# Lower parts of split weights by an adding DMA instead of a subtraction on VectorE or GpSimd

## The chip, the cores and the metric

The kernel runs on one core of a Trainium2 chip. The metric is device microseconds of one execution, the median of three runs. Beside the runs there is one profiled execution, from which the page and the trace come.

## What is computed

One layer of an encoder trunk on x of 512 x 1024 in float32: a token mixer with two branches (stick-breaking attention with 8 heads of 64, and a diagonal state-space branch, S5), their gated merge and an output projection, a layer norm, a SwiGLU channel mixer and a second layer norm. Every sub-layer is shifted, scaled and gated by vectors that come from c and w_ada. Cut to what matters:

```python
mod = silu(c) @ w_ada + b_ada              # six vectors of 1024
h = normalize(x) * (1 + sc_m) + sh_m
q, k, v, u, g_sb, g_ssm = split(h @ w_in)  # 3 x 512, 512, 2 x 1024
y_sb  = stick_breaking_attention(q, k, v) @ w_sb_up
y_ssm = s5_branch(u, ..., w_glu, b_glu) @ w_ssm_up
y = (sigmoid(g_sb) * y_sb + sigmoid(g_ssm) * y_ssm) @ w_out
x = layer_norm(ALPHA * x + (1 + g_m) * y, ln1_g, ln1_b)
h = normalize(x) * (1 + sc_f) + sh_f
gate, up = split(h @ w_ffn_in)
x = layer_norm(ALPHA * x + (1 + g_f) * (silu(gate) * up @ w_ffn_out), ln2_g, ln2_b)
```

## The kernel before

Each float32 matrix product is made of three passes in the shorter type float32r (`mm3`, L149 is its matmul). Every operand is split into an upper part, the value rounded to float32r, and a lower part, what the rounding left; the passes are upper by upper, upper by lower and lower by upper.

A weight piece of 128 x 1024 (512 KB) is a unit. `unit()` (L170) takes one of eight raw buffers, loads it on SyncE's queue, casts it on ScalarE into an upper part `whi` (L177) and subtracts the two into a lower part `wlo` (`sub`, L159) on the engine it is given. There are four `whi` and four `wlo` buffers. `slot_unit()` (L181) does the same by halves of 128 x 512 into s slots through `split()` (L164 is its cast). Which engine subtracts is written by hand: GpSimd (G) for the q and k tiles (`qk_tile`), the v tiles (`v_tiles`) and the gate tiles (`gate_tile`); VectorE (V, the default) for w_glu and the two up projections; by the table `ENG` for the twelve pieces of w_out that are split (four halved ones, and four whole ones in each of two passes over the rows), and by `FENG` for the first pairs of the channel mixer, which are two units and two halved ones. The pieces of w_ffn_out are split on VectorE; later pieces of w_ffn_in are split by `operand()` (L1049 its cast).

The stages, by the time of the profiled run: up to about 92 us the ramp, with the six vectors, the norm of x and its transposes into h (L362, L367, L368), the state-space setup (L469 among it) and the first gates; 92 to 206 us the state-space scan (L555 to L558 build the ce tiles from s tiles, L614 and L595 clear tiles, L637 to L652 are the scan) and the q, k and v tiles; 206 to 340 us attention and gate tiles (L244 accumulates the six vectors from w_ada); 340 to 350 us the copies of y (L839) and their split; 350 to 404 us the glu and the up projections; 404 to 435 us the first pass of the output projection (L916 scales rows of x on GpSimd); 435 to 472 us the first layer norm (L943, L950, L283, L284) beside the second pass; then the channel mixer and the second norm.

Each instruction belongs to a stream with a priority, in this order: first, feed, ssm, qkv, later, attn, gates, mix, ffn. Weight pieces are in feed. A scheduler places all instructions on their engines by these priorities and by its own times, so an edit of an operation moves others too. Loads keep the order of the program. Within an engine instructions run in the order placed.

Of the kernel before, what the change touches and what calls it, by code (L numbers as in the profile page):

```python
# [17 lines left out]
ALU = mybir.AluOpType  # L18
# [39 lines left out]
TAIL = 256  # L58

ENG, FENG = "VGVVVGVGGGGVVGGG", "GGGV"  # L60

# [20 lines left out]
def _build(tc, I, out):  # L82
# [75 lines left out]
    def sub(dst, a, b, eng=V):  # L158
        return eng.tensor_tensor(dst, a, b, ALU.subtract)  # L159

    def split(x, n=512, eng=V, keep=False):

        h, l = get(F32R), get(F32R)
        acopy(h[:, :n], x[:, :n])  # L164
        sub(l[:, :n], x[:, :n], h[:, :n], eng)
        if not keep:
            put(x)
        return h, l

    def unit(view, a, b, eng=V):  # L170

        with prio("feed"):
            raw = wp.tile([P, D], F32, tag="raw", name=nm("raw"), bufs=NRAW)
            load(raw.rearrange("p (a b) -> p a b", a=a), view)
            hi = wp.tile([P, D], F32R, tag="whi", name=nm("whi"), bufs=NHI)
            lo = wp.tile([P, D], F32R, tag="wlo", name=nm("wlo"), bufs=NHI)
            acopy(hi, raw)  # L177
            sub(lo, raw, hi, eng)
        return hi.rearrange("p (a b) -> p a b", a=a), lo.rearrange("p (a b) -> p a b", a=a)

    def slot_unit(view, a, b, eng=V):  # L181

# [335 lines left out]

    def fm_one(view, h, K=KC, o=None, eng=V):

        w = unit(view, K, P, eng) if K == KC else view
        o = fbank() if o is None else o
        for kc in range(K):
            mm3(o, [x[:, kc, :] for x in w], h[kc], kc == 0, kc == K - 1)
        return o
# [142 lines left out]
    def qk_tile(i):  # L668
        o = fm_one(w_in[:, :, 256 + P * i:256 + P + P * i], hT, eng=G)
        if i < 2:  # L670
# [4 lines left out]
    def v_tiles(i):  # L675
        us = [unit(w_in[:, k:k + 4, 1024 + 256 * i:1280 + 256 * i], 4, 256, G) for k in (0, 4)]
        for m2 in range(2):
# [17 lines left out]

    def gate_tile(i, eng):
        lst = (gs, gb)[i // 8]
        o = fm_one(gate_w(i), hT, eng=eng)
        with prio("feed"):
# [94 lines left out]
    for hp in range(4):  # L794
# [20 lines left out]
        for a in range(2):  # L815
# [3 lines left out]
            for g in range(2):  # L819
                i = 4 * hp + 2 * a + g  # L820
                with prio("gates"):
                    gate_tile(i, G)
                later(("gate", i))
# [74 lines left out]
    with prio("mix"):  # L898
# [10 lines left out]
        def proj(blocks):  # L909
# [7 lines left out]
            for k in range(KC):  # L917
                view, eng = w_o[:, k:k + 1, :], (V, G)[ENG[k + 8 * (blocks[0] // 2)] == "G"]
                if k >= KEEP:
                    wo[k] = [[x[:, 0, h * 512:(h + 1) * 512] for x in w] for w in [unit(view, 1, D, eng)] for h in range(2)]  # L920
                elif k not in wo:
                    wo[k] = slot_unit(view, 1, D, eng)
                later(("out", blocks[0] // 2 * 8 + k))
# [73 lines left out]
    with prio("ffn"):  # L997
        first, wx = [], []
        for i in range(FIRST):
            for c in (0, FH):  # L1000
                view = w_f[:, :, c + P * i:c + P * i + P]
                if len(first) < 2:
                    w = unit(view, KC, P, (V, G)[FENG[len(first)] == "G"])
                    w = [[x[:, k, :] for x in w] for k in range(KC)]
                else:
                    pair = slot_unit(view, KC, P, (V, G)[FENG[len(first)] == "G"])
                    wx += pair
# [171 lines left out]
        for kc in range(NF - LAST):  # L1179
            if kc == len(acts):  # L1180
                parts((kc - FIRST) // 2)
            w = unit(w_d[:, kc:kc + 1, :], 1, D)
            for m in range(NT):
# [6 lines left out]
        for kc in range(NF - LAST, NF):  # L1190
# [3 lines left out]
            if kc < NF - NHI:  # L1194
                ws[kc] = slot_unit(view, 1, D)
                order.append(kc)
            else:
                w = unit(view, 1, D)
                ws[kc] = [[x[:, 0, h * 512:(h + 1) * 512] for x in w] for h in range(2)]
# [88 lines left out]
```

## Time and profile before

| | |
|---|---|
| median of three runs | 841.67 us (841.38 to 842.21) |
| profiled execution | 841.87 us, its span 840.2 us |
| TensorE (PE) busy | 760.7 us (91%), granted clock 0.966 of full speed |
| VectorE (DVE) busy | 637.8 us (76%) |
| ScalarE (ACT) busy | 416.7 us (50%) |
| GpSimd (POOL) busy | 190.9 us (23%) |
| chain that ended last | PE 61%, DVE 24%, issue 4%, ACT 4%, DMA 4% |

The rows further below are of four views: the page (busy times, costliest groups, DMA issues), busy time by stage, and the timeline of an engine. In a timeline a line is a run of equal instructions (x tells how many), with its start, its time, and in brackets how long the engine was idle before it and what ended that.

### The profile page before, as it was taken

The numbers are of one execution on the slowest core, as the hardware profiler recorded it, in microseconds if no ns is written. First come the engines' busy times: TensorE is split into PE (matmuls) and PEld (weight loads), VectorE is DVE, ScalarE is ACT, GpSimd is POOL, SyncE is SP. The second block draws the span as 40 slices with busy tenths as digits, with TensorE's granted clock in tenths as the row PEclk, the third lists the DMA queues.
The fourth block names the chain that finished last, engine by engine and source line by source line (L and its number), as shares of the span: only waits on it lengthen the run. The fifth ranks groups of instructions, "written<-read, shape, count | busy, mean of one in ns | idle before, by whom it ended". The sixth has DMA issues, their size and how long they took to land.

```text
span 840.2 us, 12264 instructions
## 1 busy us (share of the span) xinstructions
PE 760.7 (91%) x4767; PEld 667.5 (79%) x4767; DVE 637.8 (76%) x975; ACT 416.7 (50%) x689; POOL 190.9 (23%) x161
## 2 busy tenths in 40 slices
PE   3969896899999888699998589999999999999995
PEld 2858686897888577588886589999999999888884
DVE  5599778789677998688879988767778777533267
ACT  4234623454887665883526294444445556632211
POOL 1451626662532443100464000000000000000013
PEclk9989999899999999899999699999999999999998
DMA  9960004420002471770972003414445334441001
GB/s 275 354 176 26 1 1 136 116 76 26 1 1 83 147 228 53 240 251 28 348 238 87 0 2 102 150 52 151 151 152 181 116 107 150 148 154 48 1 26 75
DMA packets 95754, 97.86 MB, mean 116 GB/s; under 512 B 4040, under 2 KB 85968, under 8 KB 95696
## 3 DMA queue, kind: packets, MB, share of 16 engines
q1 hardware_dynamic: 95552, 96.82, 36.6%
q8 instruction: 37, 0.61, 0.3%
q10 hardware_dynamic: 144, 0.26, 0.1%
q14 instruction: 21, 0.17, 0.1%
HBM read 94.97 MB, written 2.10 MB: 116 GB/s over the span
## 4 chain that ended last, share of the span: by engine, by line
PE 61%; DVE 24%; issue 4%; ACT 4%; DMA 4%; SPq 2%; POOL 1%; POOLq 0%; DVEq 0%; ACTq 0%
PE b L149 60%; DVE s L244 3%; DVE s L159 2%; SPq L146 2%; DVE s L469 1%; DMA s<-w_in 1%; DMA ra<-w_ada 1%; DVE s L621 1%; DVE wlo L159 1%; DVE raw L1042 1%; ACT s L424 1%; DVE s L642 1%; DVE s L402 1%; DVE st L280 1%; ACT s L425 1%
## 5 line engine op out<-in xcount | busy, mean ns | idle before, releaser
L149 PE MATMUL b<-h,whi 128*128 128x256 f32 (+1 forms) x896 | 217.4, 332 | 18.8 <-DVE h L159 9.4
L159 DVE TENSOR_TENSOR wlo<-raw,whi 128x1024 fp32r<-128x1024 f32 x103 | 129.5, 1264 | 69.1 <-ACT whi L177 37.1
L149 PEld LDWEIGHTS b<-h,whi 128*128 128x128 f32 x896 | 151.2, 191 | 33.4 <-DVE h L159 9.6
L149 PE MATMUL b<-s,whi 128*128 128x256 f32 (+1 forms) x800 | 166.7, 307 | 6.7 <-ACT whi L177 6.7
L149 PE MATMUL b<-h,wlo 128*128 128x256 f32 (+1 forms) x448 | 147.9, 331 | 0.0
L149 PEld LDWEIGHTS b<-s,whi 128*128 128x128 f32 x800 | 129.5, 190 | 16.6 <-ACT whi L177 7.0
L149 PE MATMUL b<-whi,s 128*128 128x512 f32 (+1 forms) x392 | 122.5, 390 | 0.0
L149 PE MATMUL b<-s,wlo 128*128 128x256 f32 (+1 forms) x400 | 121.2, 305 | 0.8 <-DVE wlo L159 0.8
L159 DVE TENSOR_TENSOR s<-s,s 128x512 fp32r<-128x512 f32 (+4 forms) x112 | 89.2, 802 | 37.0 <-PE b L149 18.1
L1049 ACT CAST whi<-raw 128x1024 fp32r<-128x1024 f32 x70 | 72.7, 1050 | 75.5 <-PE b L149 43.3
L177 ACT CAST whi<-raw 128x1024 fp32r<-128x1024 f32 x66 | 68.9, 1048 | 80.9 <-PE b L149 66.2
L159 POOL TENSOR_TENSOR wlo<-raw,whi 128x1024 fp32r<-128x1024 f32 x33 | 84.5, 2572 | 63.5 <-ACT whi L177 62.7
L149 PEld LDWEIGHTS b<-h,wlo 128*128 128x128 f32 x448 | 85.6, 191 | 7.2 <-POOL wlo L159 0.4
L1228 POOL TENSOR_TENSOR s<-s,s 128x512 f32<-128x512 f32 x6 | 8.6, 1431 | 356.6 <-DVE s L1227 356.6
L149 PE MATMUL b<-s,s 128*128 128x128 f32 (+2 forms) x438 | 81.9, 317 | 6.1 <-DVE s L159 3.8
L149 PEld LDWEIGHTS b<-whi,s 128*128 128x128 f32 x392 | 73.3, 188 | 16.6
L164 ACT CAST s<-s 128x512 fp32r<-128x512 f32 (+1 forms) x106 | 57.8, 570 | 49.4 <-DVE s L744 13.7
L149 PEld LDWEIGHTS b<-s,s 128*128 128x128 f32 x438 | 68.8, 192 | 15.9 <-DVE s L159 4.4
L149 PEld LDWEIGHTS b<-s,wlo 128*128 128x128 f32 x400 | 75.3, 188 | 4.5 <-DVE wlo L159 1.0
L149 PE MATMUL b<-wlo,s 128*128 128x512 f32 (+1 forms) x196 | 76.5, 390 | 0.0
L244 DVE SCALAR_TENSOR_TENSOR s<-ra,ca,s 128x256 f32<-128x256 f32 x88 | 58.3, 681 | 2.8 <-DMA ra<-w_ada 2.2
L159 POOL TENSOR_TENSOR s<-s,s 128x512 fp32r<-128x512 f32 (+1 forms) x32 | 39.5, 1246 | 78.9 <-ACT s L164 56.1
(244 smaller groups left out, 1111.8 us busy)
## 6 DMA issues: line engine op xcount, KB each, us to landing
raw<-w_ffn_in SPq DMA_DIRECT2D x44, 512.0 KB, 4.3
ra<-w_ada SPq DMA_DIRECT2D x32, 512.0 KB, 6.0
raw<-w_in SPq DMA_DIRECT2D x26, 512.0 KB, 4.7
raw<-w_ffn_out SPq DMA_DIRECT2D x22, 512.0 KB, 3.4
wa<-w_ada SPq DMA_DIRECT2D x12, 512.0 KB, 7.7
raw<-w_out SPq DMA_DIRECT2D x12, 512.0 KB, 6.3
s<-x SPq DMA_DIRECT2D x16, 256.0 KB, 4.2
wa<-w_ada SPq DMA_DIRECT2D x8, 256.0 KB, 4.9
```

Source lines behind the costliest of these rows:

```text
L146: return tc.keep_in_program_order(nc.sync.dma_start(out=o, in_=i))
L149: return nc.tensor.matmul(o, lhsT, rhs, start=start, stop=stop, skip_group_check=True, **kw)
L159: return eng.tensor_tensor(dst, a, b, ALU.subtract)
L164: acopy(h[:, :n], x[:, :n])
L177: acopy(hi, raw)
L244: stt(dst, r_, ca[:, k:k + 1], init if k == 0 else dst, ALU.mult, ALU.add)
L280: V.bn_stats(st[:, i, :], x)
L402: e.scalar_tensor_tensor(p_, n, -c, p_, ALU.mult, ALU.add)
L424: act(o, a, AF.Abs, bias=b)
L425: sins.append(act(o, o, AF.Sin, scale=-1.0, bias=hpi_c))
L1049: acopy(hi, x)
L1228: G.tensor_tensor(z[h], z[h], l2b[h], ALU.add)
```

## The change

A lower part is no longer raw minus upper part on VectorE or GpSimd. ScalarE writes the negated value, rounded to float32r as the upper part is, into the lower part's buffer, and a DMA issued from GpSimd adds the raw piece onto it. This is the default of `unit()` and `slot_unit()`; only w_ffn_out keeps the subtraction on VectorE, and so do `operand()` and all splits of activations, on the engines that they had. The two tables go.

```diff
-ENG, FENG = "VGVVVGVGGGGVVGGG", "GGGV"
...
+    def lower(l, x, h, eng):
+
+        if eng is None:
+            act(l, x, AF.Copy, scale=-1.0)
+            G.dma_start(out=l, in_=x, accum_op=ALU.add)
+        else:
+            sub(l, x, h, eng)
+
     def split(x, n=512, eng=V, keep=False):
 
         h, l = get(F32R), get(F32R)
         acopy(h[:, :n], x[:, :n])
-        sub(l[:, :n], x[:, :n], h[:, :n], eng)
+        lower(l[:, :n], x[:, :n], h[:, :n], eng)
...
-    def unit(view, a, b, eng=V):
+    def unit(view, a, b, eng=None):
...
             acopy(hi, raw)
-            sub(lo, raw, hi, eng)
+            lower(lo, raw, hi, eng)
...
-    def slot_unit(view, a, b, eng=V):
+    def slot_unit(view, a, b, eng=None):
...
-            w = unit(w_d[:, kc:kc + 1, :], 1, D)
+            w = unit(w_d[:, kc:kc + 1, :], 1, D, V)
...
-                ws[kc] = slot_unit(view, 1, D)
+                ws[kc] = slot_unit(view, 1, D, V)
...
-                w = unit(view, 1, D)
+                w = unit(view, 1, D, V)
```

46 units and 12 halves are concerned. The order of the loads on SyncE is the same. Elsewhere the scheduler places instructions anew; three places follow. In the names, numbers are buffers and versions; L147 is the matmul's line after the change, L149 before.

On TensorE at the first v tile (about 131 us; whi_261 and its wlo are the unit's parts, h0 and h1 the split of h), before:

```order
L149 MATMUL b4_70<-ce_179_1096,s23_185_1112 128x128
L149 MATMUL b4_70<-ce_180_1098,s16_186_1113 128x128
L149 MATMUL b7_73<-whi_261_1545,h0_64 128x256
L149 MATMUL b6_72<-whi_261_1545,h0_64 128x256
L149 MATMUL b7_73<-wlo_262_1546,h0_64 128x256
L149 MATMUL b7_73<-whi_261_1545,h1_65 128x256
L149 MATMUL b7_73<-whi_261_1545,h0_64 128x256
```

and after:

```order
L147 MATMUL b4_70<-ce_179_1098,s23_185_1114 128x128
L147 MATMUL b4_70<-ce_180_1100,s16_186_1115 128x128
L147 MATMUL b7_73<-whi_261_1551,h0_64 128x256
L147 MATMUL b6_72<-whi_261_1551,h0_64 128x256
L591 MATMUL b4_70<-ident_95,s3_136_861 128x128 x4
L147 MATMUL b7_73<-wlo_262_1552,h0_64 128x256
L147 MATMUL b7_73<-whi_261_1551,h1_65 128x256
L147 MATMUL b7_73<-whi_261_1551,h0_64 128x256
```

A row of four transposes (L591) has moved in between the first upper-part matmuls and the first one of the lower part.

On ScalarE at the start of the glu (whi_551, 560, 569 and 572 are the upper parts of the two w_glu pieces and of the first two up pieces, L839 or L845 the copies of y), before:

```order
L164 CAST s50_544_3254<-s42_535_3224 128x512
L773 COPY s40_461_2821<-b4_70 64x256
L164 CAST s48_548_3262<-s30_537_3238 128x512
L164 CAST s34_532_3208<-s40_461_2821 128x512
L177 CAST whi_551_3268<-raw_550_3266 128x1024
L177 CAST whi_560_3312<-raw_559_3310 128x1024
L177 CAST whi_569_3356<-raw_568_3354 128x1024
L177 CAST whi_572_3390<-raw_571_3388 128x1024
L847 ACT_TABLE_LOAD
```

and after:

```order
L845 COPY s41_536_3257<-b2_68 128x4x128
L845 COPY s30_537_3264<-b3_69 128x4x128
L183 CAST whi_560_3339<-raw_559_3337 128x1024
L162 ACTIVATE wlo_561_3340<-raw_559_3337 128x1024
L170 CAST s34_532_3234<-s40_461_2843 128x512
L183 CAST whi_569_3384<-raw_568_3382 128x1024
L162 ACTIVATE wlo_570_3385<-raw_568_3382 128x1024
L170 CAST s50_544_3280<-s42_535_3250 128x512
L170 CAST s45_546_3284<-s41_536_3257 128x512
L170 CAST s48_548_3288<-s30_537_3264 128x512
L183 CAST whi_572_3419<-raw_571_3417 128x1024
L162 ACTIVATE wlo_573_3420<-raw_571_3417 128x1024
```

Before, all copies and casts of y stand ahead of the first upper part; now whi_551 and its negated copy, the two rows just ahead of these, come before three copies of y, and three casts of y come after the third pair. On TensorE, at the same place, before:

```order
L149 MATMUL b6_72<-s23_542_3250,whi_560_3312 128x512
L149 MATMUL b6_72<-s39_543_3251,whi_560_3312 128x512
L149 MATMUL b7_73<-s23_542_3250,whi_560_3312 128x512
L149 MATMUL b7_73<-s39_543_3251,whi_560_3312 128x512
L149 MATMUL b4_70<-s23_542_3250,wlo_552_3269 128x512
L149 MATMUL b4_70<-s50_544_3254,whi_551_3268 128x512
L149 MATMUL b4_70<-s6_545_3255,whi_551_3268 128x512
L149 MATMUL b4_70<-s50_544_3254,wlo_552_3269 128x512
```

and after:

```order
L147 MATMUL b6_72<-s23_542_3276,whi_560_3339 128x512
L147 MATMUL b6_72<-s39_543_3277,whi_560_3339 128x512
L147 MATMUL b7_73<-s23_542_3276,whi_560_3339 128x512
L147 MATMUL b7_73<-s39_543_3277,whi_560_3339 128x512
L147 MATMUL b2_68<-s25_329_2113,whi_572_3419 128x512
L147 MATMUL b2_68<-s9_330_2114,whi_572_3419 128x512
L147 MATMUL b3_69<-s25_329_2113,whi_572_3419 128x512
L147 MATMUL b3_69<-s9_330_2114,whi_572_3419 128x512
L147 MATMUL b4_70<-s23_542_3276,wlo_552_3295 128x512
L147 MATMUL b4_70<-s50_544_3280,whi_551_3294 128x512
```

Four matmuls on the fourth upper part, whi_572, now stand ahead of the first one on the lower part wlo_552.

On ScalarE at the first layer norm (mv_677 is its first statistic, whi_663 to whi_672 pieces of w_out), before:

```order
L177 CAST whi_666_3941<-raw_665_3939 128x1024
L177 CAST whi_669_3947<-raw_668_3945 128x1024
L283 ACTIVATE mv_677_4060<-mv_677_4060,cst_102 128x1
L177 CAST whi_672_3953<-raw_671_3951 128x1024
L284 ACTIVATE mv_677_4060<-mv_677_4060 128x1
```

and after:

```order
L183 CAST whi_663_3983<-raw_662_3981 128x1024
L162 ACTIVATE s20_721_4343<-raw_717_4335 128x512
L162 ACTIVATE wlo_667_3991<-raw_665_3988 128x1024
L183 CAST whi_666_3990<-raw_665_3988 128x1024
L162 ACTIVATE wlo_670_3998<-raw_668_3995 128x1024
L183 CAST whi_669_3997<-raw_668_3995 128x1024
L162 ACTIVATE wlo_673_4005<-raw_671_4002 128x1024
L183 CAST whi_672_4004<-raw_671_4002 128x1024
L289 ACTIVATE mv_677_4112<-mv_677_4112,cst_102 128x1
L290 ACTIVATE mv_677_4112<-mv_677_4112 128x1
L953 ACTIVATE s29_675_4108<-s29_675_4108,mv_677_4112 128x512
```

Three more negated copies and one of a half now stand ahead of the first step on mv_677.

## Rows read from the trace of the kernel before

**Rows 1.** The page: busy time, share of the span and instructions of each engine.
```profile
PE 760.7 (91%) x4767; PEld 667.5 (79%) x4767; DVE 637.8 (76%) x975; ACT 416.7 (50%) x689; POOL 190.9 (23%) x161
```

**Rows 2.** Busy time by stage: from:to, length, engines, granted clock, DMA share, GB/s.
```profile
92.00:206.00 114.00, 99.32 (x635) 89.35 (x634) 95.03 (x141) 47.75 (x87) 61.23 (x52) 0.94 0.23 65
...
350.00:435.00 85.00, 85.00 (x373) 68.60 (x372) 69.62 (x107) 42.13 (x61) 18.00 (x9) 0.98 0.71 233
...
460.00:472.00 12.00, 0.50 (x2) 0.30 (x2) 12.00 (x19) 3.25 (x9) 1.93 (x5) 0.61 0.15 44
```

**Rows 3.** The page's groups: lower parts and upper parts; busy us, mean ns, idle.
```profile
L159 DVE TENSOR_TENSOR wlo<-raw,whi 128x1024 fp32r<-128x1024 f32 x103 | 129.5, 1264 | 69.1 <-ACT whi L177 37.1
...
L177 ACT CAST whi<-raw 128x1024 fp32r<-128x1024 f32 x66 | 68.9, 1048 | 80.9 <-PE b L149 66.2
L159 POOL TENSOR_TENSOR wlo<-raw,whi 128x1024 fp32r<-128x1024 f32 x33 | 84.5, 2572 | 63.5 <-ACT whi L177 62.7
```

**Rows 4.** Timeline, ramp; start, us, engine, operation, idle before in brackets.
```profile
49.28 7.82 DVE L469 TENSOR_SCALAR s<-s,s 128x128 f32<-128x128 f32 x5
...
57.88 1.11 PE L362 MATMUL b<-ident,s 128*128 128x128 f32 x4 [6.01 <-DVE s L368]
...
58.52 0.67 DVE L469 TENSOR_SCALAR s<-s,s 128x128 f32<-128x128 f32 x3
...
59.03 0.78 ACT L367 ACTIVATE h<-b,sc 128x512 fp32r<-128x512 f32 x1 [6.24 <-PE b L362]
```

**Rows 5.** Timeline, state-space part: v tiles and a wait for L558.
```profile
131.75 4.89 POOL L159 TENSOR_TENSOR wlo<-raw,whi 128x1024 fp32r<-128x1024 f32 x2 [0.44 <-ACT whi L177]
...
134.16 0.39 PE L149 MATMUL b<-wlo,h 128*128 128x256 f32 x1 [1.50 <-POOL wlo L159]
...
134.31 2.88 DVE L637 TENSOR_TENSOR s<-s,s 128x512 f32<-128x512 f32 x1
...
147.57 0.69 DVE L647 TENSOR_TENSOR s<-s,s 128x512 f32<-128x512 f32 x1
...
147.59 1.11 PE L578 MATMUL b<-ident,s 128*128 128x128 f32 x4 [4.37 <-DVE s L558]
```

**Rows 6.** Timeline, attention, VectorE and TensorE.
```profile
297.95 3.45 DVE L159 TENSOR_TENSOR s<-s,s 64x512 fp32r<-64x512 f32 x2
...
301.45 0.56 PE L149 MATMUL b<-s,s 128*128 128x256 f32 x3 [3.40 <-DVE s L159]
...
302.29 1.38 DVE L159 TENSOR_TENSOR s<-s,s 64x512 fp32r<-64x512 f32 x2
```

**Rows 7.** Timeline, start of the glu, ScalarE and TensorE.
```profile
340.88 2.90 ACT L839 COPY s<-b 128x512 f32<-128x512 f32 x3
...
348.16 1.04 ACT L177 CAST whi<-raw 128x1024 fp32r<-128x1024 f32 x1 [0.21 <-DMA raw<-w_glu]
...
349.26 3.78 PE L149 MATMUL b<-s,whi 128*128 128x512 f32 x8 [6.70 <-ACT whi L177]
352.84 0.63 PE L149 MATMUL b<-s,wlo 128*128 128x512 f32 x1
```

**Rows 8.** Timeline, output projection, GpSimd.
```profile
423.17 3.92 POOL L916 TENSOR_SCALAR s<-s 128x512 f32<-128x512 f32 x2
```

**Rows 9.** Timeline, first layer norm, VectorE.
```profile
437.05 2.28 DVE L943 SCALAR_TENSOR_TENSOR s<-s,s 128x512 f32<-128x512 f32 x1
...
456.99 2.69 DVE L159 TENSOR_TENSOR h<-s,h 128x512 fp32r<-128x512 f32 x1
...
466.67 0.68 DVE L159 TENSOR_TENSOR s<-raw,s 128x512 fp32r<-128x512 f32 x1
467.26 0.68 DVE L943 SCALAR_TENSOR_TENSOR s<-s,s 128x512 f32<-128x512 f32 x1
```

**Rows 10.** The page's DMA issues: count, KB each, median us to landing.
```profile
raw<-w_ffn_out SPq DMA_DIRECT2D x22, 512.0 KB, 3.4
wa<-w_ada SPq DMA_DIRECT2D x12, 512.0 KB, 7.7
```

More of the change, by code (lines that the diff above doesn't have):

```diff
@@ L517, in fbank, with fm_one @@
         return banks[6 + fcnt[0] % 2]
-    def fm_one(view, h, K=KC, o=None, eng=V):
-        w = unit(view, K, P, eng) if K == KC else view
+    def fm_one(view, h, K=KC, o=None):
+        w = unit(view, K, P) if K == KC else view
         o = fbank() if o is None else o
@@ L668, in qk_tile @@
     def qk_tile(i):
-        o = fm_one(w_in[:, :, 256 + P * i:256 + P + P * i], hT, eng=G)
+        o = fm_one(w_in[:, :, 256 + P * i:256 + P + P * i], hT)
         if i < 2:
@@ L675, in v_tiles @@
     def v_tiles(i):
-        us = [unit(w_in[:, k:k + 4, 1024 + 256 * i:1280 + 256 * i], 4, 256, G) for k in (0, 4)]
+        us = [unit(w_in[:, k:k + 4, 1024 + 256 * i:1280 + 256 * i], 4, 256) for k in (0, 4)]
         for m2 in range(2):
@@ L694, in _build, with gate_tile @@
     up_w = [[w[:, :, 256 * i:256 * i + 256] for w in (w_up, w_sb)] for i in range(4)]
-    def gate_tile(i, eng):
+    def gate_tile(i):
         lst = (gs, gb)[i // 8]
-        o = fm_one(gate_w(i), hT, eng=eng)
+        o = fm_one(gate_w(i), hT)
         with prio("feed"):
@@ L821, in _build @@
                 with prio("gates"):
-                    gate_tile(i, G)
+                    gate_tile(i)
                 later(("gate", i))
@@ L917, in proj @@
             for k in range(KC):
-                view, eng = w_o[:, k:k + 1, :], (V, G)[ENG[k + 8 * (blocks[0] // 2)] == "G"]
+                view = w_o[:, k:k + 1, :]
                 if k >= KEEP:
-                    wo[k] = [[x[:, 0, h * 512:(h + 1) * 512] for x in w] for w in [unit(view, 1, D, eng)] for h in range(2)]
+                    wo[k] = [[x[:, 0, h * 512:(h + 1) * 512] for x in w] for w in [unit(view, 1, D)] for h in range(2)]
                 elif k not in wo:
-                    wo[k] = slot_unit(view, 1, D, eng)
+                    wo[k] = slot_unit(view, 1, D)
                 later(("out", blocks[0] // 2 * 8 + k))
@@ L1002, in _build @@
                 if len(first) < 2:
-                    w = unit(view, KC, P, (V, G)[FENG[len(first)] == "G"])
+                    w = unit(view, KC, P)
                     w = [[x[:, k, :] for x in w] for k in range(KC)]
                 else:
-                    pair = slot_unit(view, KC, P, (V, G)[FENG[len(first)] == "G"])
+                    pair = slot_unit(view, KC, P)
                     wx += pair
```

## The prediction

> **What bounds the kernel now.** I read the page's busy times first: TensorE is busy 760.7 of 840.2 us [rows 1], so what can still be won is about 80 us of its idle time, and what can be lost is any place where it waits longer. Then busy time by stage [rows 2]: the reader should see three kinds. In 350 to 435 us TensorE has no idle time at all (85.00 of 85), so a start that comes later there goes straight to the end. In 460 to 472 us VectorE is busy without a gap (12.00) while TensorE does 0.50, so there VectorE's work is the bound. In 92 to 206 us TensorE lacks 114 − 99.32 = 14.7 us, in waits spread over the state-space part. From 522 us on nothing of the change takes place. Last, the timelines around the longest TensorE waits, to see what VectorE did while a GpSimd subtraction ran.
>
> That last view shows why the change could help. A subtraction of a lower part on GpSimd takes 2.57 us on average [rows 3], and VectorE's operation beside it does not run at its own speed. At 134.31 us a 128x512 operation of VectorE takes 2.88 us under the GpSimd pair that began at 131.75; the same shape takes 0.69 at 147.57 [rows 5]. In the ramp five 128x128 operations take 7.82 us, 1.56 each, under GpSimd's first pair, where three later ones take 0.67 in all, 0.22 each [rows 4]. At 297.95 us two 64x512 operations take 3.45 us, later two take 1.38 [rows 6]. So a GpSimd subtraction costs VectorE about 2 us, more than VectorE would need to do it itself (1.26 [rows 3]).
>
> **What is removed and added.** Counting both orders: GpSimd loses 33 subtractions of 128x1024, 33 × 2.572 = 85 us, and 4 half-size ones; VectorE loses 13 × 1.264 = 16 us and 8 half-size ones at 0.68 [rows 9]. ScalarE gains 46 negated copies of 128x1024, which I price like its cast of the same shape, 1.05 us [rows 3]: 48 us, and 12 of half size at about half, together some 55 us on an engine that is busy 416.7 of 840.2 [rows 1]. That is free only where ScalarE has room and where nothing urgent stands behind it. GpSimd's queue gains 58 DMAs. No row of before shows an adding DMA; the nearest are loads of the same 512 KB, 3.4 us at a quiet queue and 7.7 in the busy ramp [rows 10]. I take 5, because most adds fall where little is loaded, and keep 3.4 to 7.7. A lower part is thus ready about 1.05 + 5 = 6 us after its upper part instead of 2.6: 3.5 us later. A raw buffer is given back later by the same few us; SyncE's order is as before and there are eight such buffers, so I price that at nothing, and at the glu at what the range there holds.
>
> **Ramp, −4 (−6.7 to 0).** TensorE starts at 57.88 after 6.01 us of waiting for VectorE's L368 [rows 4], which stands behind the five slowed operations; they lose 7.82 − 5 × 0.22 = 6.7 us. What is late next is ScalarE: the cast of h at 59.03 [rows 4] now stands behind three upper parts and three negated copies; its last upper part ended at 52.8, 6.24 us before that cast began, so with about two copies more it is free at some 55, and some 4 us remain.
>
> **State-space part, −6 (−14.7 to 0).** Twelve of the GpSimd subtractions lie between 92 and 206 us (the pairs like 131.75's [rows 5]). One chain is shown: the 4.37 us wait at 147.59 for VectorE's L558 [rows 5] comes after four of them, each about 2 us on VectorE. Those waits for L558 should shrink by most of their length, others by a part; I take 6 of the 14.7 us that TensorE lacks there. GpSimd's own operations stand in one queue with the adds, and memsets of ce tiles there now wait for an add issued just before them; GpSimd loses 2.57 us a unit at the same time, so I price that at nothing; without that cover it is one add, 5 us, once.
>
> **v tiles, +2 (+1 to +5).** At 134.16 TensorE already waits 1.50 us for a GpSimd lower part [rows 5]. Coming 3.5 us later it would wait 5; in the new order TensorE has six instead of two matmuls ahead of it, and part of this wait lies in the shadow of the VectorE chain. I take 2.
>
> **Attention, −2 (−3.4 to +4).** VectorE loses 3.45 − 1.38 = 2.1 us just ahead of TensorE's 3.40 us wait at 301.45 [rows 6]. Against it stand gate units whose lower part comes just in time; one that is 3.5 us later could cost up to 4.
>
> **Glu, +8 (+4 to +10).** Here the order itself costs. Before, ScalarE had done its y copies (three in 2.90 us from 340.88) and the casts by the time w_glu landed, at 348.16 came the first upper part, TensorE restarted at 349.26 with eight matmuls and had its first lower part at 352.84 [rows 7]. In the new order the first upper part and its negated copy stand ahead of three of these copies, and TensorE has four matmuls on the fourth upper part (whi_572) ahead of the first lower part. From 348.16: upper and negated copy 2.1, three copies 2.9, second pair 2.1, a cast 0.5 (taken as half a 128x1024 cast), third pair 2.1, three casts 1.5, whi_572 1.05: 12.25, so 360.4. The four matmuls at the pace of the eight (3.78 / 8) take 1.9: the first lower part is used at 362.3, 9.5 later; the four are only moved, so 7.6 is lost. The adds themselves are hidden behind this: issued at about 350.3, even 7.7 us end by 358. And from here TensorE is busy without a gap until 435 [rows 2], so nothing gives it back. The low end is weights that land earlier relative to attention's end.
>
> **w_out, +2 (0 to +5).** Lower parts of the first pass are used a few us after they are ready. GpSimd's L916 operations, two in 3.92 us [rows 8], now stand between adds; one of them ahead of a needed add costs 2, two of them and a slow add 5.
>
> **First layer norm, −4 (−6 to +3).** VectorE sets the pace to 472 us. Under GpSimd's last subtractions L943 took 2.28 where the same line takes 0.68 later, and the subtraction at 456.99 2.69: 1.6 + 2.0 = 3.6 us; the half-size subtraction at 466.67 and its twin go, 1.3 [rows 9]. With one more such slowed operation that is about 6. ScalarE's first steps of the norm stand behind three more negated copies; about two of them, 2 us, are not covered.
>
> **Sum.** −4 − 6 + 2 − 2 + 8 + 2 − 4 = −4 us on the profiled run's 841.87 us (840.2 us of span and 1.67 around it), which is 0.2 above the median of 841.67: about 837.7.
>
> **A rule beside this.** Rows 5 show VectorE and GpSimd in turn rather than together. The Trainium skill, "SBUF — State Buffer", section "SBUF: two separate sides", says that the two share a port pair under an exclusive lock, and in the box on "The 'DVE blocks DMA' trap (SWDGE)" that descriptors of a DMA issued from GpSimd are written over that same pair, so that such a DMA waits while VectorE holds it. The lock agrees with rows 5; no run so far shows the second half, and the page gives 620 ns that became 3100 ns. It speaks against the change, and its mechanism is the second rival below, with prices from rows.
>
> **Rivals.** *ScalarE's order outweighs the relief: slower, 846.* The costs above, 12 us, are read from fixed orders, while the reliefs, 16 us, assume that what VectorE gains reaches TensorE. If only half does (8), the sum is 841.9 + 4 = 846. It decides as soon as less than 12 of the 16 arrive. For it: VectorE's delays lie partly where TensorE is busy anyway; against it: the waits in rows 4 to 6 end on VectorE by name. *The adds are slow: 855.* If GpSimd can issue an add only when VectorE lets it, in the stages where VectorE is busy most, each lower part comes at 7.7 us or more. Then v tiles cost 5, attention 4, w_out 5, glu 10, the norm 3, and only the ramp and a part of the state-space relief, 13 or 14, stays: 27 − 14 = +13, 855. For it: VectorE and GpSimd hinder each other in rows 4 to 6; against it: an issue is short beside a subtraction. *Relief is larger: 828.* Ramp 6.7, state-space part 10, attention 3.4, norm 6, less the same 12 us of costs: −14. For it: the slow operations form a chain; against it: ScalarE in the ramp. *Gains and costs cancel: 841 to 843*, no mechanism of its own. *The change doesn't do what it says* is excluded, since the new order holds the adds and none of the subtractions.
>
> **Numbers.** Forecast (834 to 839.9) 0.35, larger relief (826 to 834) 0.20, cancelled 0.10, ScalarE's order (843.5 to 851) 0.23, slow adds (over 851) 0.12. Faster by over 0.2% (1.7 us, about what a measurement of this kernel can tell from no change): 0.55; within: 0.10; slower: 0.35. The range leaves out the slow adds' and the larger relief's ends: 826 to 851. As both signs hold much, the likeliest case's own range is 834 to 839.9.
>
> **What would show it.** Right: VectorE's five operations at 49 us in about 1.1 us and TensorE's first start some 4 us earlier; no VectorE operation of 128x512 above 2 us between 92 and 206; waits for L558 mostly gone; TensorE's gap ahead of the glu near 12 us or more and its first glu lower part at some 8 us later after attention's end; VectorE's stretch before 472 us shorter by 4 to 6. Wrong: adds over 8 us from issue to landing, with TensorE waiting for wlo in many places; or VectorE's operations still stretched while GpSimd issues; or a glu gap as before, which would leave some 829 to 830.

## The result: slower by 2.6%

The changed kernel took 863.57 us (median of 4 runs, 860.59 to 865.57) beside 841.52 us for the kernel before: a ratio of 1.026 (95% interval 1.022 to 1.030), some 22 us more, outside the predicted range of 826 to 851. Its profiled execution has a span of 863.6 us, 23.4 more than the one before.

The page of the changed kernel, busy times, then the DMA queues (packets, MB, share of 16 engines) and the adds' median time from issue to landing:

```profile
PE 774.6 (90%) x4767; PEld 674.4 (78%) x4767; DVE 551.6 (64%) x954; ACT 463.2 (54%) x747; POOL 148.3 (17%) x182
...
q1 hardware_dynamic: 95552, 96.82, 35.5%
q0 software_dynamic: 8352, 27.27, 16.9%
...
wlo<-raw POOLq DMA_DIRECT2D x46, 512.0 KB, 5.9
```

Against [rows 1], VectorE does 86 us less (551.6), GpSimd 43 less, ScalarE 47 more. So the change did what it says, and VectorE's relief is larger than the subtractions that it lost (13 whole and 8 half ones, some 22 us). 41.3 of GpSimd's 148.3 us are now the issuing of the 46 whole adds. Still the end comes later. The new queue q0 is the adds: 27.27 MB in 16.9% of all engines' time, 0.169 × 863.6 = 146 us of all sixteen, or 2.8 us for 512 KB (52 such amounts). The loads on q1 take 0.355 × 863.6 = 307 us for 96.82 MB, 1.7 us for 512 KB. An added byte costs 1.7 times a loaded one.

Where the time goes is seen by following the same step of the program through both traces:

| step | before | after | lead (−) or lag, us | change since the row above |
|---|---|---|---|---|
| first upper-part matmul of a weight unit on h | 71.3 | 64.8 | −6.6 | −6.6 |
| first matmul on the twentieth weight unit | 261.1 | 249.3 | −11.7 | −5.1 |
| last matmul on the last gate's unit (its end) | 338.6 | 331.4 | −7.2 | +4.5 |
| first matmul on the third weight after attention (an up projection) | 362.4 | 360.8 | −1.6 | +5.6 |
| a matmul near the up projections' end (the 101st on a `whi` after attention) | 386.1 | 383.0 | −3.1 | −1.5 |
| first statistic of the first norm (VectorE) | 432.8 | 445.7 | +12.9 | +16.0 |
| first step on it on ScalarE (the logarithm) | 434.7 | 458.3 | +23.5 | +10.7 |
| end of the span | 840.2 | 863.6 | +23.4 | −0.1 |

Up to 386 us the changed kernel is ahead. Between there and the first norm's first step it loses 26.6 us. After that nothing changes between these two: the end comes 405.4 and 405.3 us after that first step. In the eighteen kernels of this study it comes 399 to 409 us after it, so the start of the norm sets the time to within some 6 us; 399.1 is e2_late's and 400.1 e4_no_ffn's, which get 5 to 6 us back behind the norm's start.

**The parts that went well.** In the ramp, where [rows 4] had five operations in 7.82 us and TensorE at 57.88, the changed kernel has (VectorE's timeline, then TensorE's):

```profile
48.80 1.06 DVE L475 TENSOR_SCALAR s<-s,s 128x128 f32<-128x128 f32 x5
```
```profile
51.36 0.66 PE L368 MATMUL b<-ident,s 128*128 128x128 f32 x4
```

And in the state-space part GpSimd issued adds at 130.35 and 132.25 while VectorE ran the scan; its operations keep their 0.69 us, where [rows 5] had 2.88 (L643 is the former L637):

```profile
129.59 0.69 DVE L643 TENSOR_TENSOR s<-s,s 128x512 f32<-128x512 f32 x1
...
132.34 1.23 DVE L648 TENSOR_TENSOR_SCAN s<-s,s 128x512 f32<-128x512 f32 x1
133.48 1.20 DVE L649 TENSOR_TENSOR_SCAN s<-s,s 128x512 f32<-128x512 f32 x1
```

**The parts that went badly.** In attention TensorE now waits for the adds, up to 2.60 us, for a lower part issued at 291.82:

```profile
299.81 0.79 PE L147 MATMUL b<-h,wlo 128*128 128x512 f32 x1 [2.60 <-DMA wlo<-raw]
```

At the glu it starts in three pieces, with waits of 3.18, 2.62 and 3.77 us in place of one of 6.70 [rows 7]. The four matmuls at 347.63 are those on the fourth weight that the new order moved ahead, so 1.5 of the 5.6 us lost here come back in the next row of the table:

```profile
337.08 2.08 PE L147 MATMUL b<-s,whi 128*128 128x512 f32 x4 [3.18 <-ACT whi L183]
341.78 2.08 PE L147 MATMUL b<-s,whi 128*128 128x512 f32 x4 [2.62 <-ACT whi L183]
347.63 2.07 PE L147 MATMUL b<-s,whi 128*128 128x512 f32 x4 [3.77 <-ACT whi L183]
349.50 0.63 PE L147 MATMUL b<-s,wlo 128*128 128x512 f32 x1
```

In the output projection the DMA engines are full. They were so before the change: the 0.71 of [rows 2] is the mean of 350 to 435 us, and within it the share is 1.00 or more from 405 to 425 us, with TensorE never idle (busy time by stage, columns as in [rows 2], the last three being granted clock, DMA share and GB/s):

```profile
405.00:415.00 10.00, 10.00 (x56) 8.05 (x55) 9.27 (x18) 6.49 (x12) 1.89 (x1) 1.00 1.02 395
415.00:425.00 10.00, 10.00 (x44) 8.08 (x43) 9.28 (x5) 3.44 (x4) 9.33 (x4) 1.00 1.00 357
```

Onto this come the adds, 59.9% of all sixteen engines from 404 to 445 us, or 25 us of their time. Busy time after the change, then the adds from the view of DMA issues of 404 to 445 us:

```profile
411.00:447.00 36.00, 28.67 (x101) 21.43 (x101) 4.46 (x8) 13.95 (x19) 10.98 (x12) 0.81 1.08 268
```
```profile
q0 software_dynamic: 1872, 4.72, 59.9%
...
wlo<-raw POOLq DMA_DIRECT2D x5, 512.0 KB, 13.1
s<-raw POOLq DMA_DIRECT2D x8, 256.0 KB, 10.2
```

Adds of 512 KB take 13.1 us in the median there from issue to landing, adds of 256 KB 10.2; in the quiet stretch from 202 to 260 us the four adds of 512 KB took 4.5. The eight adds of half pieces land about 2 us apart, from 413.7 to 427.7. TensorE on these halves, then on the second pass's:

```profile
413.12 4.36 PE L147 MATMUL b<-s,s 128*128 128x512 f32 x9 [0.53 <-DVE sfx L988]
421.10 12.68 PE L147 MATMUL b<-s,s 128*128 128x512 f32 x45 [3.62 <-ACT s L170]
...
442.51 0.50 PE L147 MATMUL b<-wlo,s 128*128 128x512 f32 x1 [1.47 <-DMA wlo<-raw]
```
```profile
447.73 8.23 PE L147 MATMUL b<-s,s 128*128 128x512 f32 x35
```

Before, 44 matmuls like those at 421 took 10.45 us, and 44 of the 48 that the second pass makes on the halved pieces came after the first pass's weights; now 35 do, so nine more of them stand ahead of the first pass's sums, and thus ahead of the norm.

These are not the only cause. TensorE's granted clock was 0.50 from 413 to 425 us, the lower of its two levels (1.2 GHz). It fell at about 412, after 32 matmuls of one column since 406.5 and a wait of 0.75 us; TensorE then waited 0.53 and 3.62 us more, and the clock was 1.00 again from 425.5, after work without a gap from 421.1. (In i1 below, which has no wait there, it falls too, but for 3 us.) In the rows of before above it is 1.00, and 44 matmuls fit into 10 us where now 18 stand in 12:

```profile
413.00:425.00 12.00, 8.26 (x18) 5.93 (x19) 0.07 (x1) 9.95 (x13) 5.97 (x7) 0.50 1.10 264
```

So the 16.0 us of the table can be divided by the two traces, up to the last matmul that VectorE needs for the first statistic (start at 429.9 before, 442.5 now): 7.3 us in which TensorE waits, some 3 for 15 more matmuls ahead of it, and some 5 because matmuls ran slower (216 in 52.2 us without the waits, before 201 in 43.8).

The last 10.7 us are lost on ScalarE. VectorE's statistic, ScalarE's timeline before the norm, and the chain of waits (start, us, what) that leads there:

```profile
447.83 0.20 DVE L287 BATCH_NORM_AGGREGATE mv<-st 128x2 f32<-128x12 f32 x1
```
```profile
437.34 1.03 ACT L183 CAST whi<-raw 128x1024 fp32r<-128x1024 f32 x1
452.06 0.63 ACT L162 ACTIVATE s<-raw 128x512 fp32r<-128x512 f32 x1 [13.69 <-DMA raw<-w_ffn_in]
...
457.34 1.03 ACT L183 CAST whi<-raw 128x1024 fp32r<-128x1024 f32 x1
458.27 0.29 ACT L289 ACTIVATE mv<-mv,cst 128x1 f32<-128x1 f32 x1
```
```profile
426.24 12.88 DMA wlo<-raw
...
439.14 3.84 SPq L144
...
443.08 8.96 DMA raw<-w_ffn_in
```

VectorE had the statistic ready at 448.0. ScalarE stood from 438.4 to 452.06 at the negated copy of half a piece of w_ffn_in, for its load. That load was issued at 443, because the load ahead of it on SyncE's queue had waited until 439 for the landing of an add of w_out that held its raw buffer (426.24 to 439.12), and issuing it then took SyncE 3.84 us. So 4.0 of the 10.2 us after the statistic are the wait for the load. The other 6.2 are the half piece's copy and six casts and copies of w_out pieces that had to stand behind it, in the order shown ahead of the prediction; only then comes the norm.

### The profile page after: what moved, and what is told of

Read it like the earlier page. It is cut to its first block, busy times and chain, and to the rows that moved or that the text cites. A ratio compares the mean times of both kernels' runs of the same rounds, so it can differ in the third digit from the quotient of the medians.

```text
span 863.6 us, 12392 instructions
## 1 busy us (share of the span) xinstructions
PE 774.6 (90%) x4767; PEld 674.4 (78%) x4767; DVE 551.6 (64%) x954; ACT 463.2 (54%) x747; POOL 148.3 (17%) x182
## 3 DMA queue, kind: packets, MB, share of 16 engines
q1 hardware_dynamic: 95552, 96.82, 35.5%
q0 software_dynamic: 8352, 27.27, 16.9%
## 4 chain that ended last, share of the span: by engine, by line
PE 46%; DMA 6%; issue 3%; DVE 3%; ACT 2%; SPq 1%; POOL 1%; POOLq 0%; DVEq 0%; ACTq 0%
PE b L147 45%; DMA wlo<-raw 2%; DMA raw<-w_ffn_in 2%; DMA s<-x 1%; SPq L144 1%; DMA raw<-w_glu 1%; DVE raw L1048 1%; DVE wlo L157 0%; DVE st L286 0%; ACT wlo L162 0%; POOL wlo L163 0%; DVE s L973 0%; DVE s L1233 0%; POOL s L157 0%; ACT s L845 0%
## 5 line engine op out<-in xcount | busy, mean ns | idle before, releaser
L147 PE MATMUL b<-h,whi 128*128 128x256 f32 (+1 forms) x896 | 221.8, 338 | 6.5 <-ACT h L979 2.6
L147 PE MATMUL b<-s,whi 128*128 128x256 f32 (+1 forms) x800 | 168.9, 310 | 9.6 <-ACT whi L183 9.6
L147 PEld LDWEIGHTS b<-h,whi 128*128 128x128 f32 x896 | 154.6, 196 | 21.8 <-ACT h L979 3.0
L147 PE MATMUL b<-h,wlo 128*128 128x256 f32 (+1 forms) x448 | 150.6, 336 | 4.2 <-DMA wlo<-raw 4.0
L157 DVE TENSOR_TENSOR wlo<-raw,whi 128x1024 fp32r<-128x1024 f32 x90 | 109.4, 1222 | 60.2 <-ACT whi L183 30.8
L147 PEld LDWEIGHTS b<-s,whi 128*128 128x128 f32 x800 | 130.4, 191 | 21.0 <-ACT whi L183 11.3
L147 PE MATMUL b<-whi,s 128*128 128x512 f32 (+1 forms) x392 | 123.7, 393 | 0.0
L147 PE MATMUL b<-s,wlo 128*128 128x256 f32 (+1 forms) x400 | 121.4, 306 | 0.4 <-DVE wlo L157 0.4
L157 DVE TENSOR_TENSOR s<-s,s 128x512 fp32r<-128x512 f32 (+4 forms) x112 | 77.8, 703 | 58.2 <-PE b L147 21.9
L147 PEld LDWEIGHTS b<-h,wlo 128*128 128x128 f32 x448 | 87.5, 195 | 12.8 <-DMA wlo<-raw 4.8
L147 PE MATMUL b<-s,s 128*128 128x128 f32 (+2 forms) x438 | 85.6, 327 | 7.1 <-ACT s L170 4.1
L147 PEld LDWEIGHTS b<-whi,s 128*128 128x128 f32 x392 | 73.9, 190 | 16.6
L147 PEld LDWEIGHTS b<-s,s 128*128 128x128 f32 x438 | 70.5, 197 | 18.8 <-ACT s L170 5.1
L147 PE MATMUL b<-wlo,s 128*128 128x512 f32 (+1 forms) x196 | 77.5, 395 | 6.2 <-DMA wlo<-raw 6.2
L147 PEld LDWEIGHTS b<-s,wlo 128*128 128x128 f32 x400 | 75.9, 190 | 4.4 <-DVE wlo L157 0.6
L163 POOL DMA_DIRECT2D wlo<-raw x46 | 41.3, 904 | 153.5 <-ACT wlo L162 138.5
L162 ACT ACTIVATE wlo<-raw 128x1024 fp32r<-128x1024 f32 x46 | 48.6, 1056 | 20.3 <-PE b L147 20.3
L1048 DVE TENSOR_TENSOR raw<-raw,raw 128x1024 f32<-128x1024 f32 x40 | 48.7, 1221 | 14.7 <-DMA raw<-w_ffn_in 14.4
```

The lines of the kernel that those rows point to most:

```text
L147: return nc.tensor.matmul(o, lhsT, rhs, start=start, stop=stop, skip_group_check=True, **kw)
L162: act(l, x, AF.Copy, scale=-1.0)
L163: G.dma_start(out=l, in_=x, accum_op=ALU.add)
L1048: tt(r, x, y, ALU.add)
```

## Experiments

In all of them a letter chooses how a lower part is made: G and V subtract on GpSimd and VectorE, A is the change (negated copy, adding DMA), C the negated copy with VectorE adding the raw piece, D a plain copying DMA with VectorE subtracting in place.

```diff
+        if eng == "A":
+            act(l, x, AF.Copy, scale=-1.0)
+            G.dma_start(out=l, in_=x, accum_op=ALU.add)
+        elif eng == "C":
+            act(l, x, AF.Copy, scale=-1.0)
+            V.tensor_tensor(l, x, l, ALU.add)
+        elif eng == "D":
+            G.dma_start(out=l, in_=x)
+            V.tensor_tensor(l, l, h, ALU.subtract)
+        else:
+            sub(l, x, h, eng)
```

The diffs below change the letters of QK (q and k), VT (v), GATE, GLU, UP, WO (pieces 0 to 3 halved, 4 to 7 and 12 to 15 whole) and FE (first four of w_ffn_in). Before they are G, G, sixteen G, V, V, "VGVVVGVGGGGVVGGG", "GGGV"; after all are A.

### Early or late?

```diff
-QK, VT, GATE = "G", "G", "G" * 16        (e1_early, from the kernel before)
+QK, VT, GATE = "A", "A", "A" * 16
-WO, FE = "VGVVVGVGGGGVVGGG", "GGGV"      (e2_late, from the kernel before)
+WO, FE = "A" * 16, "A" * 4
-FE = "A" * 4                             (e4_no_ffn, from the changed kernel)
+FE = "GGGV"
```

> Adding DMAs only for the 26 units of q, k, v and the gates; all later weights subtracted as in the kernel before. Theory A (the loss sits in the output projection and the first norm, where adds of w_out and w_ffn_in fill the DMA engines and hold raw buffers; the gain before 260 us comes from GpSimd's subtractions being gone): TensorE is about 10 to 12 us ahead at 260 us, gives back about 3 in attention, and keeps the rest: 831 to 836 us. Theory B (the loss is spread, each add costs a little everywhere): 845 to 850 us.

> Adding DMAs only for the twelve pieces of w_out and the first four of the channel mixer; everything earlier as before. Theory A: nothing changes up to 404 us, then the output projection loses some 12 us and the first norm some 11: 860 to 867 us. Theory B: 845 to 850 us.

> As the changed kernel, but the four first pieces of w_ffn_in are subtracted on GpSimd and VectorE as before. Theory A with ScalarE standing at a negated copy for a late w_ffn_in load (13.7 us at 452 us in the changed kernel) as the norm's loss: the first step of the norm comes about 8 to 10 us earlier, 852 to 857 us. Rival: the norm's loss is from the w_out adds alone: 860 to 865 us.

e1_early took 831.67 us, ratio 0.989 (0.986 to 0.993); e2_late 859.78, 1.022 (1.020 to 1.025); e4_no_ffn 850.76, 1.012 (1.008 to 1.015). Theory A holds for the place: early adds gain 9 us, late ones lose 19. Early adds with the rest as before beat the kernel before. e4_no_ffn gives back 12.8 of the 22 us, more than expected: in the traces 7.8 by the norm's first step and 5 behind it.

### What makes the early gain?

```diff
-QK, VT, GATE, WO, FE = "G", "G", "G" * 16, "VGVVVGVGGGGVVGGG", "GGGV"   (e3_all_v)
+QK, VT, GATE, WO, FE = "V", "V", "V" * 16, "V" * 16, "V" * 4
```

> No adding DMA and no subtraction of weights on GpSimd: VectorE does them all, at 1.22 us each. If the gain before 260 us comes from GpSimd's subtractions no longer stretching VectorE's operations by about 2 us each, TensorE is 8 to 12 us ahead at 260 us here too, and the run takes 829 to 836 us. Rival: the gain needs the work to leave VectorE's queue altogether; then 838 to 846 us.

It took 827.84 us, ratio 0.984 (0.981 to 0.987), faster than e1_early, though its late pieces differ too. Its busy times:

```profile
PE 762.5 (92%) x4767; PEld 669.5 (81%) x4767; DVE 613.3 (74%) x1012; ACT 416.0 (50%) x689; POOL 104.5 (13%) x124
```

VectorE does 37 more subtractions (33 whole ones of 1.23 us among them, some 43 us in all) and is busy 24.5 us less than before (637.8 [rows 1]). So, by this sum, GpSimd's 37 subtractions had cost VectorE about 67 us, some 2 us each, as [rows 4 to 6] suggested. Between 92 and 206 us the kernel before has twelve VectorE operations of over 1.9 us; this one has none, nor has the changed kernel. The gain of the change is the absence of GpSimd's work; the DMAs are not needed for it.

### DMA time, or ScalarE's copies?

```diff
-WO, FE = "VGVVVGVGGGGVVGGG", "GGGV"
+WO, FE = "C" * 16, "C" * 4               (f1_copy_no_dma)
+WO, FE = "D" * 16, "D" * 4               (f2_plain_dma)
+WO = "C" * 16                            (h1_wout_copy)
+WO = "A" * 16                            (h3_wout_add)
+FE = "A" * 4                             (h2_ffn_add)
+FE = "C" * 4                             (h4_ffn_copy)
```

> As e2_late (w_out and the first pieces of w_ffn_in), with the same negated copies on ScalarE, but VectorE adds the raw piece instead of a DMA. Theory A (DMA time and late landing): without the DMAs the output projection and the first norm lose nothing of the kind, 838 to 846 us. Rival (ScalarE's added copies and the order they force): they stay, so 854 to 860 us.

> As e2_late, but GpSimd issues a plain copying DMA of the raw piece into the lower part's buffer, with no accumulation, and VectorE then subtracts the upper part in place; no negated copies on ScalarE. If the accumulation makes the adds slow (in the changed kernel an add of 512 KB took 2.8 us of all 16 engines' time against 1.7 for a load), the copies take about 1.7, land in 6 to 8 us instead of 13 to 16 in the output projection, and the run takes 844 to 850 us. If any transfer within SBUF from GpSimd's queue is as slow, they land as late, 856 us or more.

> Negated copy on ScalarE and addition on VectorE for w_out alone, everything else as before. If the DMA engines' time is what the output projection loses, and the first pieces of w_ffn_in what the norm loses, this stays near the kernel before: 840 to 846 us. Rival: ScalarE's twenty more copies in the output projection cost by themselves; 850 us or more.

> Adding DMAs for w_out alone. Theory A: the output projection loses some 10 to 13 us by adds that land 10 us and more after their issue, and the norm nothing more: 851 to 855 us. Rival: parts add up otherwise, since e2_late lost 19 us and e4_no_ffn 10: under 847 us, with the loss only where w_ffn_in adds follow.

> Adding DMAs for the first four pieces of w_ffn_in alone. Here a negated copy of a half piece stands on ScalarE between the first step of the norm's statistic and its first scaling, and waits for a load. If this standing in the queue is the norm's loss, some 5 to 12 us: 846 to 853 us, and the norm starts late. Rival: the loss needs the w_out adds ahead of it, which make the loads late; then 840 to 844 us.

> Negated copy on ScalarE and addition on VectorE for the first four pieces of w_ffn_in alone, no DMA. With the copy standing in ScalarE's queue ahead of the norm's scaling as the cause, this loses what h2_ffn_add loses, within 3 us. With the adds' DMA time as the cause it is near the kernel before: 840 to 844 us.

| kernel | median us | ratio (95%) | from the matmul near the up projections' end to the first statistic, us | statistic ready to first step on ScalarE, us |
|---|---|---|---|---|
| before | 841.5 | | 46.8 | 0.4 |
| e1_early | 831.7 | 0.989 (0.986 to 0.993) | 46.3 | 0.4 |
| h2_ffn_add | 837.1 | 0.996 (0.994 to 0.998) | 46.8 | 0.4 |
| h4_ffn_copy | 840.8 | 1.000 (0.998 to 1.001) | 46.8 | 0.4 |
| f2_plain_dma | 853.5 | 1.015 (1.010 to 1.020) | 55.9 | 0.0 |
| h1_wout_copy | 852.1 | 1.013 (1.010 to 1.016) | 56.7 | 0.0 |
| f1_copy_no_dma | 852.1 | 1.013 (1.010 to 1.016) | 57.3 | 0.0 |
| h3_wout_add | 856.5 | 1.018 (1.016 to 1.021) | 62.7 | 1.4 |
| e4_no_ffn | 850.8 | 1.012 (1.008 to 1.015) | 62.4 | 2.6 |
| e2_late | 859.8 | 1.022 (1.020 to 1.025) | 63.0 | 10.0 |
| after | 863.6 | 1.026 (1.022 to 1.030) | 62.7 | 10.2 |

Theory A, that DMA time alone is what the output projection loses, falls in f1 and h1: without any such DMA, negated copies with VectorE's additions lose 10 of the 16 us (f1's time lies between its two expected ranges, h1's in the rival's). In h1 TensorE has no wait over 1 us there; it does other work first:

```profile
440.28 7.13 PE L149 MATMUL b<-s,s 128*128 128x512 f32 x30
```

Only 30 of those 44 matmuls of the second pass are left after the first pass; 14 have moved ahead of the norm's sums, and VectorE's additions stand among the norm's steps. Divided as for the changed kernel, h1's 9.9 us are 1.7 of TensorE's waiting, some 4 for 18 more matmuls ahead, some 2 by slower matmuls (clock 0.83 from 417 to 424 us), and 2.7 of VectorE's own: two additions of 1.23 us stand around the steps that lead to the statistic. These 2.7 us the changed kernel does not have (its VectorE needs 0.2 us more than before), so the two losses are only in part the same.

The adds (h3) cost 6 us more than these copies (62.7 against 56.7): TensorE waits 2.2 us more, and its matmuls take some 3.5 us more, at a granted clock of 0.50 from 417 to 424 us where h1 has 0.83. The queues of e2_late and f2_plain_dma tell the price of accumulation, for the same bytes; the median is over all ten whole pieces:

```profile
q0 software_dynamic: 3168, 8.39, 5.2%
...
wlo<-raw POOLq DMA_DIRECT2D x10, 512.0 KB, 9.2
```
```profile
q0 software_dynamic: 3168, 8.39, 2.9%
...
wlo<-raw POOLq DMA_DIRECT2D x10, 512.0 KB, 7.0
```

5.2% against 2.9%: 2.8 us of all engines for 512 KB against 1.5. A plain copy takes about as much as a load, an add 1.8 times a copy. But plain copies land late too: the first four whole ones, issued into the burst from 411 to 417 us, took 13.8 to 16.4 us from issue to landing, where 6 to 8 had been expected, and e2_late's first four adds 14.4 to 19.2. So an add's price alone does not make it late. f2's run was no faster than f1's, but it differs in VectorE's work too.

That w_ffn_in's own pieces lose time falls as well: h2 and h4 lose nothing, h2 gains 4 us, which neither expectation had. Their copy stands in ScalarE's queue there too, but its load has come. The 10 us of standing need both: adds of whole w_out pieces, which hold raw buffers, and behind them copies of w_ffn_in. It is 10.0 to 10.3 us in the three kernels that have both (after, e2, i2 below) and at most 2.6 in those that have one or none.

### Which pieces of w_out?

```diff
-WO = "A" * 16                            (from the changed kernel)
+WO = "VGVVVGVGGGGVVGGG"                  (i1_wout_as_before)
+WO = "VGVV" + "A" * 12                   (i2_halves_as_before)
+WO = "AAAA" + "VGVGGGGVVGGG"             (i3_wholes_as_before)
```

> The changed kernel with w_out subtracted as before; adding DMAs everywhere else. If w_out is the whole cause, the lead of the early part remains (e1_early: 9 us) less what the adds of the glu and the up projections cost (3 to 4 us), and the w_ffn_in adds cost nothing, as in h2_ffn_add: 831 to 838 us. Rival: the w_ffn_in pieces lose their own 10 us, since ScalarE stands at a negated copy for their load here too: 842 to 850 us.

> The changed kernel with only the four halved pieces of w_out subtracted as before; the eight whole ones by adding DMAs. If the eight adds of half pieces, landing 2 us apart, pace TensorE and start the loss, most of it goes: 840 to 848 us. If the whole pieces with their copies on ScalarE and the order they bring do it: 853 us or more.

> The changed kernel with the eight whole pieces of w_out subtracted as before; the four halved ones by adding DMAs. If the half pieces' adds start the loss: 850 us or more. If the whole ones do it: 838 to 846 us.

i1 took 844.52 us, ratio 1.005 (1.003 to 1.007); i2 855.28, 1.018 (1.014 to 1.022); i3 847.56, 1.009 (1.007 to 1.011). So w_out makes 19 of the 22 us, but not all. The time lies in the range of the rival, but the rival's mechanism is not there: the statistic waits 0.4 us for ScalarE. Instead, i1 is 13 us slower than e1_early, of which 2 are lost by the up projections' end, 3.5 between there and the norm's first statistic, and 3 after the norm's first step; the other 4 of the gap between the medians do not show in the two profiled executions. The whole pieces weigh more (16 us back without their adds) than the halves (8), and both together give back 19, less than the sum; i3, still 7 us slower than the kernel before, lies between its two expected ranges. In i2, where the whole pieces are added and the copies of w_ffn_in follow, the standing on ScalarE is there, the statistic having been ready at 441.2:

```profile
445.28 0.63 ACT L165 ACTIVATE s<-raw 128x512 fp32r<-128x512 f32 x1 [12.42 <-DMA raw<-w_ffn_in]
...
451.49 0.29 ACT L301 ACTIVATE mv<-mv,cst 128x1 f32<-128x1 f32 x1
```

In i3, with the halves added and the whole pieces subtracted, the statistic waits 0.6 us.

### Versions that beat both

```diff
+QK, VT, GATE = "V", "V", "V" * 10 + "A" * 6; WO, FE = "V" * 16, "V" * 4      (g1_v_then_add)
+QK, VT, GATE = "A", "V", "A" * 16;           WO, FE = "V" * 16, "V" * 4      (g2_add_then_v)
+QK, VT, GATE = "V", "V", "V" * 16;           WO, FE = "V" * 16, "A" * 4      (i4_v_ffn_add)
```

> All subtractions of weights on VectorE, but the last six gate units, which fall into attention where VectorE is busy, by adding DMAs. The all-VectorE kernel (827.8) loses its lead of 27 us at some 225 us down to 14 in attention. If VectorE's own subtractions cost that, 822 to 826; if adds are as late there as in the changed kernel (8 us), 828 to 832.

> Adding DMAs for q, k and the gates, VectorE subtractions for v, the glu, the up projections, w_out and the first pieces of w_ffn_in. The early part as e1_early, 7 us ahead at the up projections, the late part as in e3_all_v, where the lead over the kernel before stayed about what it was: 831 to 834 us; below e3_all_v only if adds beat VectorE in the early part.

> No subtraction of weights on GpSimd: VectorE does all of them, but the first four pieces of w_ffn_in by adding DMAs. The all-VectorE kernel took 827.8 us and adds for w_ffn_in alone gained 4 us on the kernel before; if that is VectorE's time in the norm, 822 to 826 us; if it was GpSimd's hold on VectorE there, which is gone already, 826 to 830 us.

g1 took 827.81 us, ratio 0.985 (0.981 to 0.989); g2 830.79, 0.988 (0.984 to 0.992); i4 826.00, 0.983 (0.981 to 0.985). The early adds are no better than VectorE's own subtractions (g2 against 827.84 of e3_all_v), nor are they in attention (g1). Adds for the four w_ffn_in pieces may be worth 2 us; the intervals of i4 and e3 overlap, and i4 stands on the border of its two expected ranges, so h2's gain stays unexplained. The fastest is i4, with VectorE doing nearly everything: its first step of the norm comes 13.5 us before that of the kernel before.

```profile
421.25 0.29 ACT L301 ACTIVATE mv<-mv,cst 128x1 f32<-128x1 f32 x1
```

## Why the prediction was wrong

Step by step, with the forecast and what the table of the two traces shows:

- **Ramp**, −4 (−6.7 to 0): −6.6. The five operations took 1.06 us as counted, and ScalarE stood next in line as counted, but its three pairs ran without a gap and the cast of h came at 53.69, not at 55.
- **State-space part and v tiles**, −6 and +2: −5.1 together up to the twentieth unit. Right. VectorE keeps its speed while GpSimd issues adds, and TensorE's three waits for L558 (7.9 us in all) are gone; a new one of 3.84 us, for ScalarE at 133.6, takes half of that back.
- **Attention**, −2 (−3.4 to +4): +4.5, just outside. The lower parts that come just in time were the larger effect: two waits for adds, 4.0 us in all; adds took 6.8 us there in the median.
- **Glu**, +8 (+4 to +10): +5.6, or 4.1 with the four matmuls that were only moved. The mechanism was right, and its place: copies of y behind the first pairs on ScalarE.
- **w_out**, +2 (0 to +5): +16.0. This step failed. The sum priced an add at 5 us, from loads, and one GpSimd operation ahead of it. It missed four things. The DMA engines were full in this stage already (1.00 to 1.02 from 405 to 425 us before), and the sum has no term for 25 us more of their time: adds queue behind each other and behind loads (13.1 us). The order, which I compared on ScalarE, had moved second-pass matmuls ahead of the first pass's sums on TensorE; I looked at TensorE's order only at the v tiles and the glu. Around TensorE's waits its clock stood at 0.50 for 12 us, worth some 5 us, in a stage that had 1.00 before. And the low slack of these pieces made every such delay count.
- **First norm**, −4 (−6 to +3): +10.7. This step failed too. I saw the copy of the half piece of w_ffn_in ahead of the norm's first step and counted it as one copy more. What counts is what it waits for: a load that SyncE issues only when an add has landed and given back its raw buffer. The sentence that priced the later return of raw buffers at nothing was the wrong one; its cover, eight buffers, was gone as soon as 13 us passed between issue and landing.

Of the rivals, the slow adds (855 us) came nearest, in its result and in its price of an add; not in its mechanism. There GpSimd was to issue adds only when VectorE let it. The issue took 0.85 us in the middle of VectorE's work, and the adds issued in the quiet 202 to 260 us landed in 4.5 us with VectorE busy 58% of the time. There is one exception, in the ramp (GpSimd, then VectorE):

```profile
54.08 1.97 POOL L163 DMA_DIRECT2D wlo<-raw  x1 [0.79 <-ACT wlo L162]
```
```profile
54.87 0.76 DVE L401 TENSOR_SCALAR s<-s 128x512 f32<-128x512 f32 x2
55.54 0.43 DVE L402 TENSOR_SCALAR s<-s 128x512 f32<-128x512 f32 x1
```

This issue took 1.97 us, and ended 0.1 us after three VectorE operations with one input, which took 0.43 us each for a shape that takes 0.69 with two. The same happens at this place in e1, e4, g2 and i1 (1.8 to 1.9 us, ending 0.1 us after the third). It delays one add by 1 us and explains nothing of the loss. So of the rule in the Trainium skill, "SBUF — State Buffer" (section "SBUF: two separate sides"), this case supports the first half, the two engines in turn, in [rows 5] and in e3_all_v's 24.5 us less of VectorE with more to do; for the second half, that VectorE starves the descriptors of such a DMA, the one issue of 1.97 us is a sign, and beside VectorE's operations with two inputs, as at 130 us, there is none.

The first rival, ScalarE's order, was half right: in w_out the copies without any DMA lose 10 us (h1, f1), though 2.7 of these are VectorE's additions and no run separates ScalarE's order from TensorE's.

Open: how much of the late landing in w_out is the add's higher price and how much the number of transfers that meet full DMA engines; plain copies in f2 landed late too. Also why h2 gains 4 us, and what the order on TensorE alone is worth: holding the order fixed while changing the operation was not tried, so the divisions of the w_out loss above are read from traces and not tested by a run.

## What to carry to other kernels

When a step moves from an engine to a DMA, ask what the DMA's landing gives back (a buffer, a queue's turn), and follow that to the loads behind it and to whatever in-order engine stands in front of them: here 13 us in a raw buffer became 10 us before a layer norm that had nothing to do with it. Price a DMA in the stage where it will run, beside the loads there and beside the others of its kind, not from a quiet one; look at the DMA share of that very stretch first (here 1.00, hidden in a mean of 0.71), since a full stretch has no room for more. And a stretch with waits of TensorE can cost more than the waits: here 7.3 us of them went with some 5 us of slower matmuls. And before moving work off an engine that is being slowed by another, try simply taking it away from the one that slows it: VectorE with all subtractions was faster than VectorE with fewer.

## What the runs showed of the hardware

- An adding DMA within SBUF took 2.8 us of all 16 engines for 512 KB, a copying one 1.5 and a load 1.7; in a quiet stretch it landed 4.5 us after issue, in the changed kernel's burst 13 to 16 us; copying ones took 14 to 16 in theirs.
- GpSimd was occupied 0.85 us by issuing an adding DMA of 512 or 256 KB, and 0.53 by a copying one; VectorE's operations beside it kept their time. In the ramp one issue took 1.8 to 2.0 us in five kernels, ending 0.1 us after three VectorE operations with one input (128x512 in 0.43 us).
- A 128x1024 subtraction on GpSimd (2.57 us) takes about 2 us from VectorE, which does the same subtraction in 1.23.
- In the changed kernel TensorE's granted clock fell to 0.50 at about 412 us, around waits of 0.75, 0.53 and 3.62 us, and came back at 425.5, after work without a gap from 421.1; in the kernel before, without waits, it was 1.00 through that stretch, and in i1, also without, it fell for 3 us.
